# Gates taken out of PSUM by tanh and product, scores held 2^7 larger, and gate transposes moved into another PSUM tile, in a two-layer streaming encoder step

## The chip, the cores and the metric

The kernel runs on one core of one Trainium2 chip. A core has five engines that work side by side, each on its own queue of instructions in a fixed order: TensorE (PE in the profile; its weight loads are shown apart as PEld), VectorE (DVE), ScalarE (ACT), GpSimd (POOL), and SyncE (SP), which here issues the transfers (DMA). TensorE writes its results to PSUM, a small memory of banks, from where ScalarE and VectorE read them; everything else lies in SBUF. The metric is the device time of one execution in microseconds (us); the time given for a kernel is the median over its runs.

## The reference

Two layers run one after the other over a prompt of 2048 tokens and a sample of 64 tokens (width 1024, heads of 64). Each layer is, cut to what matters:

```python
h = rms_norm(x, norm_g)
q, k, v, gate = split(h @ w_in)                 # one combined projection
q, k = rms_norm per head (q, q_g), (k, k_g)
s = q @ k.T * 64 ** -0.5 + bias                 # own chunk of 64 and the chunks before it
p = softmax(s)                                  # layer A: with a sink per head in the sum
y = x + ((p @ v) * silu(gate)) @ w_out
```

Layer A has 16 query heads over 2 key/value heads and looks back 128 tokens; its bias is bucketed by distance. Layer B has 16 heads of each and looks back 512 tokens; its bias comes from a clipped distance. The outputs are the two results and the last rows of keys and values. silu(g) = g / (1 + exp(-g)) = 0.5 g (1 + tanh(g / 2)); the kernel uses the second form.

## The kernel before

All tokens are split into units of 256 (u0 to u7, two tiles of 128 each) and the sample as a unit of its own, which is taken ahead of the last one (`order`). Layer A works through its heads in four groups (qd 0 to 3), layer B through eight head pairs (hp 0 to 7), each over all units. A projection has its own PSUM tile (`project`, tag pj, a ring of two): chains of matmuls over eight blocks of the input, each with high and low parts of the operands, which come from ScalarE (copy) and VectorE (rest): `load_weights`, lines 467 and 470.

**The order of the work.** Attention is a pipeline over units, written out as steps: one step is the scores of one tile and one head (`scores`), and around it stands what is due. Between these the projections of later units are dealt out a few matmuls at a time (`filler.to`), so that TensorE always has something to do; the small works of a unit (head norms, gates, scans of the weights) stand in a list with a cost each (`Background`) and are handed out at each step (`bg.share`) or when the unit's scores need them. The order on each engine is then settled by a planner that simulates the program; each engine takes its queue in that order and waits on the others by semaphores.

**The gates.** When a projection is done, `evacuate` (layer A, 256 gate columns of 512) and `evacuate_b` (layer B, 128 of 512, for two tiles per unit) bring it out of PSUM. ScalarE copies queries and keys to `a` (tile pa; lines 702 and 715) with the token's scale, and the gate to tile pb (L702 also, and L723); in layer B it takes the values in between (L719, their rest on VectorE, L720). `head_norm` squares and sums queries and keys (GpSimd L756, VectorE L757 or L765, GpSimd L760, L761, and L769) and scales them (VectorE L774). `gate`, one of the works of the background list, then makes tanh(g/2) on ScalarE (L782) and (tanh + 1) g on VectorE (L783). In layer B the scale of the copy is C_B, one of three numbers per pair in `scl`, which `everywhere` spreads over the partitions from a row that `input_across` works out (the weights' largest values come from scans, L175).

**Attention in layer B, pairs 1 to 7.** Scores go to a PSUM tile with tag sb (1024 columns), a ring of two (L1416, L1417). One VectorE instruction per tile and head adds the bias and takes the minimum (L1420; the scores are held negative), ScalarE takes the exponent and its sum (L1429). The order in a unit is tile 0 and 1 of head 0, then of head 1. Head 0's probabilities are turned by a DMA transpose (`TURNED = (0,)`: ScalarE L1463 and GpSimd L1464 split them); head 1's on TensorE, one step after their scores, into another sb tile, from which ScalarE and VectorE take a high and a low part (`values`: L844 by way of `transpose`; L816, L817). I call these fillings PT01 (tile 0 of head 1) and PT11 (tile 1), and the scores' tiles S00, S10, S01, S11. Once the last row of a unit's sums is there, VectorE takes the reciprocal (L1437), multiplies head 0's part by PB (L1440) and GpSimd multiplies the gates by it into G (L1448, two instructions). Some steps later, in the rest of head 1's `products`, `gates` takes another sb tile, TensorE turns G into it (L844 again), ScalarE copies it with scale G_B (L1237), and `finish_pairs` multiplies it into the output (ScalarE L1247, VectorE L1249, GpSimd L1250). `store_kv` makes the output keys on GpSimd (L795). Pair 0 and layer A use another PSUM tile (tag tp) for the turned gates, and in layer A the scores' minimum is L1150.

**Constants.** `constants` loads the gains of queries and keys and works out their powers of two on VectorE: the keys' share `kf`, the queries' `qf`, while the weights of the first projection are being split.

Of the kernel before, what the change touches and what calls it, by code (L numbers as in the profile page):

```python
# [56 lines left out]
def hybrid_encoder_kernel(  # L57
# [71 lines left out]
    kf = const([P, 2], "kf")  # L129
    kgr = const([P, 2, 2 * HD], "kgr")  # L130
# [3 lines left out]
    held = {}  # L134

    def constants():
# [8 lines left out]
        nc.vector.tensor_tensor(qf, qsc, ksc, op=ALU.mult)  # L145
        nc.vector.tensor_scalar(kf.bitcast(I32), qf.bitcast(I32), 0x7F800000, None, op0=ALU.bitwise_and)
        nc.vector.tensor_scalar(kf, kf, 0.125, 1.0, op0=ALU.mult, op1=ALU.max)
        nc.vector.tensor_scalar(kf, kf, 2.0 ** 15, 1.0, op0=ALU.min, op1=ALU.mult)
        inv = t("ms", [P, 8])[:, 0:2]
        nc.vector.reciprocal(inv, kf)  # L150
        nc.vector.tensor_tensor(qf, qf, inv, op=ALU.mult)
        nc.vector.tensor_scalar(qf, qf, 60000.0, -60000.0, op0=ALU.min, op1=ALU.max)
# [5 lines left out]
    scl = const([P, 9, 3], "scl")  # L158
    gsb = const([P, 8, KC], "gsb")
    S_W, C_B, G_B = (lambda h, i=i: scl[:, h, i : i + 1] for i in range(3))  # L160
# [24 lines left out]
    def times(dst, a, c):  # L185
        nc.vector.tensor_scalar(dst, a, c, 1.0, op0=ALU.mult, op1=ALU.mult)

# [22 lines left out]
    def everywhere(h, o):  # L210
        ps = psum("tp", 512, 1)
        nc.tensor.matmul(ps[:, 0:3], ones[0:1, 0:1].to_broadcast([1, P]), o, start=True, stop=True)
        nc.vector.tensor_copy(scl[:, h], ps[:, 0:3])
# [6 lines left out]
    def input_across(h):  # L220
        across(h, h + 1)
        e, r, o = row[:, 16:17], row[:, 17:18], row[:, 20:23]
        powers(row[:, h : h + 1], e, r)
        times(o[:, 0:1], r, WB_)
        times(o[:, 1:2], e, 1 / (HB * WB_))
        times(o[:, 2:3], e, 0.5 / VB if h > 0 and len(TURNED) == 2 else 0.5 / (VB * PB))

    def input_scales(h):
        everywhere(h, row[:, 20:23])
        nc.vector.tensor_scalar(gsb[:, h], gain[:, 1, :], S_W(h), 1.0, op0=ALU.mult, op1=ALU.mult)  # L230
# [57 lines left out]
    def bias_vectors_a():  # L288
# [4 lines left out]
        nc.vector.tensor_scalar(va[:16, :VL], ps[:16, :VL], -1.0, 1.0, op0=ALU.mult, op1=ALU.mult)  # L293

    def bias_vectors_b():
# [5 lines left out]
            vb[:16, 127:383], vr[:16, 0:256], vr[:16, 0:1], -1.0, op0=ALU.subtract, op1=ALU.mult  # L301
        )

# [118 lines left out]
    bg = Background()  # L422

# [185 lines left out]
    rr = [const([P, NT + 1], f"rms{l}") for l in range(2)]  # L609

# [8 lines left out]
    def sums_to_scales(layer, tt, parts, ps):  # L619
# [12 lines left out]
        )  # L632

# [12 lines left out]
    def row_scales(unit):  # L646
# [18 lines left out]
        nc.gpsimd.tensor_tensor(rr[0][:, tt : tt + w], v[:, :w], mhalf[:, :w], op=ALU.pow)  # L665

# [21 lines left out]
    def evacuate(layer, tt, n, ps, C, G, b=None):  # L688
        a = t("pa", [P, 384], 4)
        pieces = [(a[:, : C - G], ps[:, : C - G])]  # L690
        if G:
            out = a
            if b is None:
                b = t("pb", [P, 256], 5)
                out = a, b
            pieces.append((b[:, :G], ps[:, C - G : C]))
        else:
            out = a
        sc = rr[layer][:, tt : tt + 1]
        for dst, src in pieces:  # L700
            if n == P:
                held["evac"] = nc.scalar.activation(dst, src, AF.Identity, scale=sc).ins  # L702
            else:
                nc.scalar.activation(dst[:n], src[n:], AF.Identity, scale=sc[n:])
        if n < P:
            for dst, src in pieces:
                nc.vector.scalar_tensor_tensor(
                    dst[:n], src[:n], sc[:n], dst[:n], op0=ALU.mult, op1=ALU.add
                )
        return out  # L710

    def evacuate_b(hp, tt, ps, g):
        a = t("pa", [P, 384], 4)
        true = a if tt >= NT - 4 else a[:, 0:256]
        nc.scalar.activation(true, ps[:, : true.shape[1]], AF.Identity, scale=C_B(hp))  # L715
# [7 lines left out]
        held["evac"] = nc.scalar.activation(g, ps[:, 384:512], AF.Identity, scale=C_B(hp)).ins  # L723
# [122 lines left out]
    halves = [slice(0, 64), slice(64, 128)]  # L846

# [1074 lines left out]
```

## Time and profile before

| what | value |
|---|---|
| runs | 2204.73, 2210.4 and 2212.95 us; median 2210.4 us |
| profiled execution | 2214.94 us |
| its span, first to last instruction | 2213.1 us (1.8 us lie around it) |
| TensorE busy | 2102.7 us, 95% |
| VectorE, ScalarE, GpSimd busy | 1563.9 (71%), 1425.7 (64%), 1004.9 us (45%) |
| TensorE's granted clock, mean | 0.991 |
| layer A, projections and attention | 6 to about 690 us; first scores at 47.3 |
| layer A's output projection | about 650 to 885 us |
| layer B, pair 0 | about 885 to 1050 us |
| layer B, pairs 1 to 7 | about 1050 to 2065 us |
| layer B's output projection | to 2209 us |

How the lines are read: a group of instructions shows its line in the kernel, its engine, its operation, output tile <- input tiles, shape and count, then busy time and mean ns of one, then the idle time of the engine ahead of them and who ended it. A row of waits shows engine, tile and line, "<-" the engine, tile and line that it waited for, and total us, number, longest us. A row of the timeline shows start, duration, engine, line and operation, and in brackets the idle time before it and who ended that. A row of a stretch shows the length, and for PE, PEld, DVE, ACT and POOL the busy time and the number of instructions, then granted clock, DMA share and GB/s.

### The profile page before, as it was taken

The page shows a single profiled execution, that of the slowest core. Times are in us where ns is not written, and L with a number is a line of the kernel's source. Part 1 is how long each engine was busy: PE and PEld are TensorE (multiplying, and loading weights), DVE is VectorE, ACT ScalarE, POOL GpSimd, SP SyncE. Part 2 cuts the span into 40 slices and gives each one's busy share as a digit, 9 for nine tenths or more (in the row PEclk, how much of TensorE's full clock was granted, in tenths as well). Part 3 has the DMA queues.
Part 4 walks back from the last instruction along what each step waited for, and adds up shares of the span by engine and source line. Part 5 has one row for each costly group of instructions (what it writes and reads, how often), then busy time and mean ns, then how long its engine had stood idle before and what let it go on. Part 6 is the DMA issues. An engine that isn't in the chain of part 4 may idle for free. (4 is left out here: it accounts for less than half of the span.)

```text
span 2213.1 us, 41369 instructions
## 1 busy us (share of the span) xinstructions
PE 2102.7 (95%) x13441; PEld 1522.1 (69%) x13441; DVE 1563.9 (71%) x4105; ACT 1425.7 (64%) x3610; POOL 1004.9 (45%) x1509
## 2 busy tenths in 40 slices
PE   7999999999999999989999999999999998998999
PEld 6887888788889997556555555555555555556888
DVE  6769777677676456778676777877767778677642
ACT  6878878777785333666666766766667667576420
POOL 5645544334454455853444444444454445443000
PEclk9999999999999999999999999999999999999999
DMA  8856546856546667545465565654756546345664
GB/s 274 275 162 215 179 127 219 234 160 195 170 129 184 210 204 244 171 143 167 107 186 133 130 177 130 173 148 121 186 133 155 159 111 172 91 104 136 199 200 124
DMA packets 383096, 372.87 MB, mean 168 GB/s; under 512 B 174672, under 2 KB 320352, under 8 KB 382848
## 3 DMA queue, kind: packets, MB, share of 16 engines
q1 hardware_dynamic: 382880, 370.23, 58.0%
q8 instruction: 106, 1.74, 0.3%
q14 instruction: 110, 0.90, 0.1%
HBM read 257.59 MB, written 73.43 MB: 150 GB/s over the span
## 5 line engine op out<-in xcount | busy, mean ns | idle before, releaser
L679 PE MATMUL pj<-wh,xx 128*128 128x512 f16 (+2 forms) x1648 | 643.4, 390 | 5.8 <-ACT pb L702 4.1
L681 PE MATMUL pj<-wh,xx 128*128 128x512 f16 (+2 forms) x1648 | 625.5, 380 | 2.5 <-POOL xx L564 2.5
L680 PE MATMUL pj<-wh,xx 128*128 128x512 f16 x1024 | 391.5, 382 | 0.0
L1429 ACT ACTIVATE p<-p,nm 128x640 f32<-128x640 f32 (+5 forms) x264 | 198.9, 753 | 213.6 <-DVE nm L1420 108.0
L1765 PE MATMUL pj<-xx,wh 128*128 128x264 f32 (+1 forms) x1024 | 290.0, 283 | 8.5 <-DVE res L1775 4.1
L1766 PE MATMUL pj<-xx,wh 128*128 128x264 f32 (+1 forms) x1024 | 287.7, 281 | 0.0
L1464 POOL TENSOR_TENSOR values<-p,values 128x640 f16<-128x640 f32 (+2 forms) x112 | 140.0, 1250 | 243.5 <-ACT values L1463 243.5
L680 PE MATMUL pj<-wl,xx 128*128 128x512 f32 (+1 forms) x624 | 233.9, 375 | 2.2 <-DVE wl L470 2.2
L564 POOL TENSOR_TENSOR xx<-xraw,xx 128x528 fp32r<-128x528 f32 (+4 forms) x144 | 184.9, 1303 | 87.8 <-ACT xx L563 74.6
L1420 DVE CUSTOM_DVE_ANT_0 p<-sb,BT 128x640 f32<-128x640 f32 (+5 forms) x272 | 195.6, 719 | 38.3 <-PE sb L1417 35.6
L1250 POOL TENSOR_TENSOR o<-gt,o 128x256 f32<-128x256 f32 (+1 forms) x132 | 101.1, 766 | 206.2 <-ACT p L1156 89.6
L761 POOL TENSOR_TENSOR f<-f,mhalf 128x4 f32<-128x4 f32 (+2 forms) x187 | 187.0, 1000 | 13.8
L681 PEld LDWEIGHTS <-xx 128*128 128x128 f16 x1024 | 100.9, 99 | 125.9 <-issue 3.9
L774 DVE TENSOR_TENSOR pa<-pa,f 128x256 f32<-128x256 f32 (+3 forms) x221 | 136.5, 618 | 55.1 <-POOL f L761 50.6
L1156 ACT ACTIVATE p<-p,nm 128x257 f32<-128x257 f32 (+2 forms) x272 | 134.3, 497 | 50.1 <-DVE nm L1150 41.7
L756 POOL TENSOR_TENSOR sq<-pa 128x256 f32<-128x256 f32 (+2 forms) x187 | 123.7, 663 | 72.5 <-ACT pa L715 38.2
L679 PEld LDWEIGHTS <-xx 128*128 128x128 f16 x1024 | 101.0, 99 | 71.5 <-issue 2.7
L680 PEld LDWEIGHTS <-xx 128*128 128x128 f16 x1024 | 100.9, 99 | 70.3 <-issue 2.9
L817 DVE SCALAR_TENSOR_TENSOR pl<-sb,ph 128x640 f16<-128x640 f32 (+4 forms) x144 | 106.2, 737 | 58.2 <-ACT ph L816 56.5
L1767 PE MATMUL pj<-xx,wl 128*128 128x264 f32 x512 | 145.0, 283 | 1.0 <-DVE wl L463 1.0
L1767 PE MATMUL pj<-xx,wh 128*128 128x264 f16 x512 | 142.1, 277 | 1.3 <-DVE wh L460 1.3
L1150 DVE CUSTOM_DVE_ANT_0 p<-sa,BT,nsink 128x256 f32<-128x256 f32 (+2 forms) x272 | 117.3, 467 | 34.6 <-PE sa L844 29.5
(273 smaller groups left out, 5290.7 us busy)
## 6 DMA issues: line engine op xcount, KB each, us to landing
xx<-xsb SPq DMA_DIRECT2D x112, 512.0 KB, 4.2
xx<-xsa SPq DMA_DIRECT2D x88, 512.0 KB, 4.8
xraw<-oga SPq DMA_DIRECT2D x64, 264.0 KB, 3.6
xraw<-ogb SPq DMA_DIRECT2D x64, 264.0 KB, 3.6
xsa<-xx SPq DMA_DIRECT2D x32, 512.0 KB, 4.0
scan<-in_w_in_b_dram SPq DMA_DIRECT2D x64, 256.0 KB, 4.6
wl<-in_w_in_b_dram SPq DMA_DIRECT2D x64, 256.0 KB, 4.0
xraw<-in_x_dram SPq DMA_DIRECT2D x40, 256.0 KB, 3.9
```

The costliest lines, as they stand in the source:

```text
L564: nc.gpsimd.tensor_tensor(lo, rv, wide(hi), op=ALU.subtract)
L679: nc.tensor.matmul(ps[:n, :C], xh, wh, start=k == 0, stop=False)
L680: nc.tensor.matmul(ps[:n, :C], xh, wl, start=False, stop=False)
L681: nc.tensor.matmul(ps[:n, :C], xl, wh, start=False, stop=k == KC - 1)
L761: nc.gpsimd.tensor_tensor(fv, fv, mhalf[:n, :H], op=ALU.pow)
L774: nc.vector.tensor_tensor(sv, sv, fv.unsqueeze(2).to_broadcast([n, H, HD]), op=ALU.mult)
L1420: mi = nc.vector.tensor_tensor_reduce(out=p[r, :nk], in0=S[r, o : o + nk], in1=b, op0=ALU.add, op1=ALU.min, scale=1.0, scalar=3e38, accum_ ...
L1429: ex = nc.scalar.activation(p[:n, :nk], p[:n, :nk], AF.Exp, scale=-1.0, bias=it.nm[:n, c : c + 1], accum_out=it.sm[:n, c : c + 1],)
L1464: lo = nc.gpsimd.tensor_tensor(two[:, :, 1, :], pv, two[:, :, 0, :], op=ALU.subtract)
L1765: nc.tensor.matmul(ps[:, :OT], wh, oh, start=k == 0, stop=False)
L1766: nc.tensor.matmul(ps[:, :OT], wh, ol, start=False, stop=False)
L1767: nc.tensor.matmul(ps[:, :OT], wl, oh, start=False, stop=k == KC - 1)
```

## The change

It has three parts.

1. Gates. In full tiles, `evacuate` and `evacuate_b` no longer copy the gate: a new `gate_of` takes tanh on ScalarE straight from PSUM, and VectorE multiplies (tanh + 1), or (tanh - 1) in layer A, with the PSUM tile into its place. In layer A the token scale is then missing; half of its negative (`nhalf`) is the tanh's scale, and the reciprocal sums `sm` are multiplied by the token scale and -1. In layer B, `scl` has a fourth number H_B, and C_B squared goes into G_B. `evacuate_b` does the gate first, then the copy to pa, then the values. The background work `gate` remains for the sample alone.
2. Scores. Queries are scaled by `up`, at most 2^7, a power of two found from the gains (the gains are loaded a second time, to every partition, 128x4, 256 KB); the biases are scaled by -up (`nup`), and the minimum instructions scale by `down` = 1/up from a [P, 1] pointer in place of the number 1.0. The factor PB goes into `scl` once per pair, and the multiplication after the reciprocal (L1440) goes.
3. Gate transposes of pairs 1 to 7. They go from the rest of the products, where they had an sb tile of their own, to the filling PT11, ahead of its transposes of probabilities, in columns 640 to 895 of the same tile; the copy (`gate_t`) follows the split of the probabilities.

```diff
+    def gate_of(ps, scale, g, one=1.0):
+        W = g.shape[1]
+        e = t("e", [P, 256], 1)[:, :W]
+        held["evac"] = nc.scalar.activation(e, ps, AF.Tanh, scale=scale).ins
+        nc.vector.scalar_tensor_tensor(g, e, one, ps, op0=ALU.add, op1=ALU.mult)
...
+        if n == P:
+            held["evac"] = nc.scalar.activation(a[:, : C - G], ps[:, : C - G], AF.Identity, scale=sc).ins
+            if G:
+                gate_of(ps[:, C - G : C], nhalf[:, tt : tt + 1], b[:, :G], -1.0)
+            return (a, b) if G else a
...
     def evacuate_b(hp, tt, ps, g):
         a = t("pa", [P, 384], 4)
         true = a if tt >= NT - 4 else a[:, 0:256]
+        gate_of(ps[:, 384:512], H_B(hp), g)
         nc.scalar.activation(true, ps[:, : true.shape[1]], AF.Identity, scale=C_B(hp))
...
-        held["evac"] = nc.scalar.activation(g, ps[:, 384:512], AF.Identity, scale=C_B(hp)).ins
         return a
...
+        both = t("res", [P, 2 * OT], 2)[:, : 4 * P].rearrange("p (d c) -> p d c", c=4)
+        load(both, qk_gain.partition_broadcast(P))
+        nc.vector.tensor_tensor(both[:, :, 0:2], both[:, :, 0:2], both[:, :, 2:4], op=ALU.mult)
+        nc.vector.tensor_reduce(
+            up, both[:, :, 0:2].rearrange("p d c -> p c d"), axis=AX.X, op=ALU.max,
+            apply_absolute_value=True,
+        )
+        exponent(up, up)
+        nc.vector.tensor_scalar(up, up, 2.0 ** 10, 1e-20, op0=ALU.mult, op1=ALU.max)
+        nc.vector.reciprocal(up, up)
+        nc.vector.tensor_scalar(up, up, 2.0 ** 29 * 2.0 ** 7, 2.0 ** 7, op0=ALU.mult, op1=ALU.min)
+        nc.vector.reciprocal(down, up)
+        times(nup, up, -1.0)
+        nc.vector.tensor_tensor(qsc, qsc, up, op=ALU.mult)
...
-                        op0=ALU.add, op1=ALU.min, scale=1.0,
+                        op0=ALU.add, op1=ALU.min, scale=down[:n, 0:1],
...
             nc.vector.reciprocal(sm[:n], sm[:n])
+            if n == P:
+                nc.vector.tensor_scalar(
+                    sm, sm, rr[0][:, tt : tt + 1], -1.0, op0=ALU.mult, op1=ALU.mult
+                )
...
-                    op0=ALU.add, op1=ALU.min, scale=1.0, scalar=3e38, accum_out=it.nm[r, c : c + 1],
+                    op0=ALU.add, op1=ALU.min, scale=down[r, 1:2], scalar=3e38, accum_out=it.nm[r, c : c + 1],
...
-                if turned(it, 0) and len(TURNED) == 1:
-                    part = it.sm[:n, TURNED[0] : w : 2]
-                    nc.vector.tensor_scalar(part, part, PB, 1.0, op0=ALU.mult, op1=ALU.mult)
...
+            gates_too = u != NU and it.hp > 0 and (i, h) == (1, 1)
+            if gates_too:
+                GT = PT[:, 5 * P : 5 * P + T]
+                for e, (_, g0, _) in enumerate(tiles):
+                    transpose(GT[:, g0 : g0 + n], it.G[:n, e * P : (e + 1) * P])
             for c in range(m):
                 transpose(PTv[:, (kb + c) % 5, :n], it.p[i, h][:n, c * P : (c + 1) * P])
...
+            if gates_too:
+                it.gt = gate_t(GT.rearrange("p (j s) -> p j s", j=1), T, G_B(it.hp))
...
             def rest():
-                if h == 1:
+                if h == 1 and it.hp == 0:
                     gates(it)
```

89 lines of the change are left out of this document (51 added, 38 removed).

## The prediction

> **What bounds the kernel now.** I read the first part of the page for the busiest engine, then the same engine by stage, then what its idle time ended on, and last, in the timeline, the places where it stops.
>
> ```profile
> span 2213.1 us, 41369 instructions
> PE 2102.7 (95%) x13441; PEld 1522.1 (69%) x13441; DVE 1563.9 (71%) x4105; ACT 1425.7 (64%) x3610; POOL 1004.9 (45%) x1509
> ```
>
> TensorE is busy for 95% of the span; the next engine, VectorE, for 71%. The change leaves the number and the shapes of the matmuls and transposes as they are, so it can only move TensorE's waits: 2213.1 - 2102.7 = 110 us, 6.4 of it before the first matmul and 3.8 behind the last. By stretches (layer A's beginning; layer B's head pair 0; its pairs 1 to 7):
>
> ```profile
> 0.00:200.00 200.00, 182.15 (x1091) 153.45 (x1092) 143.90 (x518) 155.05 (x415) 112.10 (x169) 0.98 0.73 231
> 885.00:1050.00 165.00, 152.81 (x932) 92.10 (x931) 131.40 (x300) 109.04 (x272) 94.96 (x127) 0.99 0.50 160
> 1050.00:2065.00 1015.00, 957.52 (x5976) 583.81 (x5975) 757.11 (x1948) 682.65 (x1705) 470.18 (x704) 0.99 0.55 142
> ```
>
> The columns are the length, then busy time and count of PE, PEld, DVE, ACT and POOL, and the granted clock (0.98 to 0.99 throughout). TensorE is idle 17.8 us in the first stretch, 12.2 in pair 0, and 57.5 in pairs 1 to 7, some 8 per pair. That last is the most there is to win where most of the change lies. What ended TensorE's waits, as total, times, longest:
>
> ```profile
> PE sb L844 <- DVE nm L1420: 14.0, 7, 2.3
> PE sb L1416 <- DVE nm L1420: 12.7, 10, 1.7
> PE tp L844 <- DVE pa L774: 11.0, 8, 1.7
> PE sb L844 <- DVE pl L817: 10.2, 14, 1.4
> PE pj L679 <- ACT pb L702: 4.1, 3, 2.1
> PE sb L844 <- ACT gt L1237: 1.5, 3, 0.9
> ```
>
> **1. Gates out of PSUM (evacuate, evacuate_b).** Before: ScalarE copies the gate to SBUF (L702, L723), later a tanh in SBUF (L782) and a VectorE product of two SBUF tiles (L783). After: tanh straight from PSUM, and a product that reads PSUM.
>
> ```profile
> L783 DVE SCALAR_TENSOR_TENSOR pb<-sq,pb 128x128 f32<-128x128 f32 x128 | 55.6, 434 | 20.5 <-ACT sq L782 20.3
> L723 ACT ACTIVATE pb<-pj,scl 128x128 f32<-128x128 f32 x128 | 46.6, 364 | 63.7 <-DVE values L720 60.9 <-DVE scrow L202 1.2
> L782 ACT ACTIVATE sq<-pb 128x128 f32<-128x128 f32 x128 | 38.4, 300 | 0.6
> L720 DVE SCALAR_TENSOR_TENSOR values<-pj,values 128x128 f16<-128x128 f32 x128 | 36.5, 285 | 2.9 <-ACT values L719 1.4
> L702 ACT ACTIVATE pb<-pj,rms 128x256 f32<-128x256 f32 x64 | 30.1, 470 | 0.0
> L782 ACT ACTIVATE sq<-pb 128x256 f32<-128x256 f32 x64 | 26.8, 419 | 2.8 <-DVE f L765 1.6
> L1237 ACT ACTIVATE gt<-sb,scl 128x256 f32<-128x256 f32 x56 | 26.2, 467 | 0.3
> ```
>
> I take the PSUM tanh at the price of the copy that it replaces, so ScalarE loses the L782 groups: 38.4 + 26.8 = 65 us. The product from PSUM is nearest to L720 (one PSUM and one SBUF input, 285 ns); L783 costs 434 because it varies from 258 to 1514 ns:
>
> ```profile
> L783 DVE SCALAR_TENSOR_TENSOR pb<-sq,pb x204: 258/411/1514, 35.0 to 2014.1; 128x128 f32<-128x128 f32 x64, 128x256 f32<-128x256 f32 x32, 128x64 f32<-128x64 f32 x4, 64x256 f32<-64x256 f32 x2
> L720 DVE SCALAR_TENSOR_TENSOR values<-pj,values x128: 268/286/293, 873.6 to 2009.4; 128x128 f16<-128x128 f32 x128
> ```
>
> So VectorE saves 128 x 0.149 = 19 us in layer B (bounds 0 and 19). [...]
>
> Neither engine sets the end, so the 65 and 19 us are worth only what they take from TensorE's waits (3 below). Against them stands a later release. In layer A the projection's PSUM tile (pj, two in a ring) now goes free behind a VectorE product instead of a ScalarE copy: 256 wide some 0.42 us, and up to one other VectorE instruction (0.6) ahead of it, +0.4 to +1.2. TensorE already waits there (row L679 <- L702: 4.1 us in 3) while head norms and projections come densely, up to 200 us; later such tiles are 3 us and more ahead. 3 waits x 0.6, and some 1 us at places that are now just covered: **+3 (0 to +6)**. The 17 small halvings on POOL and 64 scalings of sm on VectorE (L1440's kind, 178 ns) lie beside other work: 0.
>
> In layer B the order becomes tanh, product, pa copy, V; before it was pa copy, V, gate. The row of L723 shows that two readers of a pj tile take turns: ScalarE stood 60.9 us, 55 times, behind VectorE's L720 on the same tile. So the pa copy starts 0.36 (tanh) + 0.29 (product) + up to 0.6 (VectorE's queue) = 0.65 to 1.25 later; were both engines free to read, 0.36. [...]
>
> What hangs on pa are head norm, the tp transposes, and the scores. The chain has slack in most units; not at a pair's last unit, whose second tile stops TensorE (L844 <- L774, 11.0 us in 8). There VectorE itself stands behind a scan's transfer:
>
> ```profile
> 1327.06 0.29 DVE L783 SCALAR_TENSOR_TENSOR pb<-sq,pb 128x128 f32<-128x128 f32 x1 [0.46 <-ACT sq L782]
> 1329.36 0.69 DVE L175 TENSOR_REDUCE most<-scan 128x1 f32<-128x512 f32 x1 [2.01 <-DMA scan<-in_w_in_b_dram]
> 1330.93 0.84 DVE L1249 TENSOR_TENSOR o<-o,o 64x256 f32<-64x256 f32 x2
> ```
>
> L774 follows L175, so a later pa is covered by those 2.01 us; in the changed order two L1249 (0.84 together) come ahead of the second L774 and one L783 (0.28) goes: **+0.5 per pair (0 to +0.9)**. Pair 0, where VectorE is busy for 131 of 165 us: **0 (-3 to +3)**, its lighter queue against its later pa.
>
> **2. Scores 2^7 larger (scale=down).** The minimum instructions take the scale from a pointer. The nearest rows are the two layers' own forms: L1150 already has one pointer more than L1420.
>
> ```profile
> L1150 DVE CUSTOM_DVE_ANT_0 p<-sa,BT,nsink 128x128 f32<-128x128 f32 x16 | 5.0, 346 | 2.4 <-PE sa L844 1.5 <-POOL f L769 0.9
> L1420 DVE CUSTOM_DVE_ANT_0 p<-sb,BT 128x128 f32<-128x128 f32 x16 | 4.6, 285 | 10.1 <-PE sb L1417 10.1
> L1440 DVE TENSOR_SCALAR sm<-sm 128x2 f32<-128x2 f32 x56 | 10.0, 178 | 1.3
> ```
>
> 61 ns each (0 to 61), x 256 in layer B = 16 us of VectorE, against 10.0 for L1440, which goes (PB is put into scl once per pair), and the 19 above: VectorE is about 13 us lighter in layer B.
>
> The beginning is different. The constants load 256 KB more (both), ahead of the weights on the SP queue, and VectorE gets two instructions of 256 elements and a net six tiny ones, in a stretch in which TensorE waits for VectorE's weight halves:
>
> ```profile
> 15.18 0.16 DVE L152 TENSOR_SCALAR qf<-qf 128x2 f32<-128x2 f32 x1
> 16.91 0.41 DVE L591 TENSOR_TENSOR o<-res 128x256 f32<-128x256 f32 x1
> 27.39 0.50 PE L680 MATMUL pj<-wl,xx 128*128 128x512 f32 x1 [2.19 <-DVE wl L470]
> 47.29 0.26 PE L1139 MATMUL sa<-KA,q 128*128 128x128 f16 x1 [3.86 <-ACT values L789]
> ```
>
> 2 x 0.41 + 6 x 0.16 = 1.8 us, which go straight to TensorE, whose waits of 2.19 and, ahead of the first scores, 3.86 us stand behind this stretch; a late transfer can add as much again where VectorE waits for it, and idle moments can hide half: **+3 (+1 to +5)**.
>
> **3. Gate transposes into the filling of PT11 (pairs 1 to 7).** Before, each unit used the ring of two sb tiles 7 times, the gate's (then L1237 on ScalarE) among them; after, 6 times. The waits for L1237 go (1.5 us in 3): **-0.2 per pair**. The new wait: the transposes stand at the front of the filling with the unit's last probabilities, one step behind its last scores, and need G, two POOL products behind the reciprocal. How early is G today? In order, a unit 1, 3, 4 and 5 of one pair:
>
> ```profile
> 1225.37 0.76 POOL L1448 TENSOR_TENSOR G<-pb,sm 128x128 f32<-128x128 f32 x2 [1.45 <-DVE sm L1440]
> 1226.22 0.60 PE L844 MATMUL sb<-ident,p 128*128 128x128 f32 x4
> ...
> 1258.74 1.29 POOL L1448 TENSOR_TENSOR G<-pb,sm 128x128 f32<-128x128 f32 x2 [1.59 <-DVE sm L1440]
> 1260.68 0.76 PE L844 MATMUL sb<-ident,p 128*128 128x128 f32 x5 [1.05 <-DVE pl L817]
> ...
> 1276.90 0.46 POOL L795 TENSOR_TENSOR ko<-pa,kgr 128x128 f32<-128x128 f32 x1 [0.58 <-DVE pa L774]
> 1277.53 0.76 POOL L1448 TENSOR_TENSOR G<-pb,sm 128x128 f32<-128x128 f32 x2 [0.17 <-PE sb L844]
> 1276.73 0.71 PE L844 MATMUL sb<-ident,p 128*128 128x128 f32 x5
> ...
> 1291.80 1.01 POOL L761 TENSOR_TENSOR f<-f,mhalf 128x4 f32<-128x4 f32 x1
> 1293.45 1.39 POOL L1448 TENSOR_TENSOR G<-pb,sm 128x128 f32<-128x128 f32 x2
> 1295.47 0.74 PE L844 MATMUL sb<-ident,p 128*128 128x128 f32 x5 [2.31 <-DVE nm L1420]
> ```
>
> G ends 0.09 us ahead of the filling in unit 1 (1226.13 against 1226.22), 0.65 in unit 3, 0.63 in unit 5, and 1.56 behind it in unit 4 (1278.29 against 1276.73). With L1440 gone G comes some 0.2 earlier. In unit 4 the changed order puts G ahead of L795 on POOL, which takes off 0.46 + 0.17 more: a wait of about **+0.7 per pair (0 to +1.6)**.
>
> In unit 5, 2.31 us end on scores whose PSUM tile frees late, since ScalarE reaches the copy of the tile (L816) with a backlog; of that one L1237 (0.47) and one L782 (0.30) go. But G is only 0.63 + 0.2 ahead there: no more than 0.83 can be won of the 2.31, and in unit 3 no more than 0.85 of its 1.05, since then the filling waits for G. I take **-0.7** in unit 5 and **-0.4** in unit 3. The gate's copy now stands behind VectorE's L817 of the same tile, which holds the tile some 0.5 longer; its next user comes 3 us later: 0.
>
> **Sum.** Per pair +0.5 - 0.2 + 0.7 - 0.7 - 0.4 = -0.1, over 7 pairs -1 (-13 to +12). Beginning +3, layer A +3, pair 0 0: **+5**. The profiled execution took 2214.9 us (span 2213.1 and 1.8 around it) and would be 2220; the median of the runs is 4.5 lower, 2210.4, so I predict **2215**.
>
> **Rivals.**
> - **G is late (slower).** If VectorE's pointers (61 ns x 4 per unit) eat what L1440 gives back, and L795 still stands ahead, unit 4 waits the whole 1.56: net +0.75 a pair, 5 us, +6 elsewhere, 11 over the median; from that point on it decides. Half a microsecond later still adds 0.4 each in units 1 and 7 and 0.5 in unit 4; one POOL power instruction ahead of G (1.01 us) makes 5.5 a pair. In between, some 3.5 x 7 + 6 = +30: **2240**. For it: POOL takes turns with long instructions; against it: in the other units POOL already waits for L1440 (the bracketed 1.45 and 1.59) and so would start G sooner.
> - **The relief pays (faster).** ScalarE's 65 and VectorE's 13 us take the waits in units 3 and 5 down to where G stops them, 0.85 + 0.83, and gt's 0.2: 1.9 x 7 = 13, and the beginning costs only 1: **2198**. It needs G in unit 4 to be in time, 1.56 earlier; the rows give 0.8 to 1.0.
> - **pa's lateness shows.** Unit 7 +0.9 x 7, pair 0 +4, layer A +6, beginning +3: **2229**. For it: the turns on the pj tile; against: the 2.01 us of the scan that cover it.
> - **Nothing shows**: all beside TensorE, **2210**.
>
> **Chances.** Forecast 0.46 (own range 2204 to 2226), G late 0.22, relief 0.17, pa 0.10, nothing 0.05. Half a per cent, 11 us, is about what a measurement of this kernel can tell from no change. From the cases: slower 0.05 + 0.20 + 0.07 = 0.32, faster 0.16, within 0.52. The range takes the relief and half of G late: **2194 to 2238**.
>
> **What would show it.** Right: L782's 128-wide groups gone, the product near 285 ns with a small spread, no TensorE wait for gt, a wait of TensorE's sb transposes for POOL's G once per pair (unit 4) near 0.7, pj waits in the first 200 us longer by 2 to 4, and the first scores later than 47.3 us by 2 to 4. Wrong: G waits in most units (slower), or pairs 1 to 7 idle under 45 us (faster).

## The result, and the profile after

The changed kernel takes 2224.5 us (median of six runs, 2221.1 to 2227.9) against 2209.1 us for the kernel before (six runs, 2204.7 to 2213.3): a ratio of 1.0068, 95% interval 1.0049 to 1.0086, so 15 us slower. The predicted 2215 was 9.5 us short, and the range held the time.

The page of the changed kernel begins:

```profile
span 2223.7 us, 41231 instructions
PE 2107.8 (95%) x13441; PEld 1526.4 (69%) x13441; DVE 1573.5 (71%) x4146; ACT 1384.1 (62%) x3418; POOL 997.2 (45%) x1518
```

TensorE has the same 13441 instructions and is as full as before; ScalarE has 192 fewer. The waits of TensorE, as total, times, longest:

```profile
PE tp L884 <- DVE pa L814: 22.1, 8, 8.7
PE sb L1460 <- DVE nm L1464: 11.6, 15, 1.7
PE tp L884 <- DVE scl L236: 8.4, 5, 1.7
PE sb L884 <- POOL G L1489: 6.2, 15, 0.5
PE sb L884 <- DVE pl L857: 6.0, 7, 1.8
PE pj L717 <- DVE pb L730: 3.9, 4, 1.5
PE sb L884 <- DVE nm L1464: 3.6, 2, 2.0
```

Against the rows before: the waits on the head norm (pa) doubled from 11.0 to 22.1 us, with one of 8.7 among them; a small copy (scl) went from 1.3 to 8.4; G is new with 6.2; the waits for the turned tile's release (L884 <- L1464, 14.0 before) and for pl (10.2) shrank; gt's is nearly gone.

Where the time went, stage by stage, from the start times of TensorE's instructions in the two traces (a stage runs from its first scores to the next stage's, the last one to the start of the last matmul; "idle" is the sum of TensorE's gaps over 0.06 us in it, "rest" is its length less that):

| stage | before: idle + rest, us | after: idle + rest, us | change, us |
|---|---|---|---|
| to the first scores | 13.7 + 33.6 | 15.2 + 37.9 | +5.8 |
| layer A, to its last scores | 9.4 + 620.7 | 10.8 + 619.3 | 0.0 |
| to pair 0's first scores | 10.8 + 203.3 | 9.5 + 205.9 | +1.3 |
| pair 0 | 12.2 + 148.1 | 20.6 + 152.2 | **+12.5** |
| pairs 1 to 7, to the last scores | 57.5 + 942.3 | 52.8 + 938.6 | -8.4 |
| to the last matmul | 3.1 + 154.4 | 2.7 + 154.1 | -0.7 |

The stages sum to +10.5 us, the difference of the two profiled executions. The other 5 us of the median are not in them: the profiled execution of before was 5.9 us above its median of six, that of after 1.0.

**Pair 0.** Here lies nearly all of the growth of the waits on the head norm. In pair 0 alone, before and then after:

```profile
PE tp L844 <- DVE pa L774: 1.4, 2, 0.9
PE tp L884 <- DVE pa L814: 12.4, 2, 8.7
```

The two waits of the changed kernel are 8.73 us and, 21 us later, 3.69 us. The timeline of the changed kernel at the longer one, GpSimd first, then VectorE and TensorE:

```profile
902.95 0.80 POOL L796 TENSOR_TENSOR sq<-pa 128x256 f32<-128x256 f32 x1
906.33 1.27 POOL L591 TENSOR_TENSOR xraw<-xraw,rows 128x512 f32<-128x512 f32 x1 [2.59 <-DMA xraw<-x]
907.56 1.15 POOL L595 TENSOR_TENSOR xx<-xraw,xx 128x512 f16<-128x512 f32 x1
908.67 0.20 POOL L800 TENSOR_TENSOR f<-f,small 128x4 f32<-128x4 f32 x1
908.82 3.37 POOL L595 TENSOR_TENSOR xx<-xraw,xx 128x512 f16<-128x512 f32 x3
912.14 1.01 POOL L801 TENSOR_TENSOR f<-f,mhalf 128x4 f32<-128x4 f32 x1
913.19 0.83 DVE L814 TENSOR_TENSOR pa<-pa,f 128x256 f32<-128x256 f32 x1 [3.59 <-POOL f L801]
914.16 0.66 PE L884 MATMUL tp<-ident,pa 128*128 128x128 f32 x2 [8.73 <-DVE pa L814]
```

The head norm's two small steps (L800, L801; 1.2 us together) stand on GpSimd behind a product that waits 2.6 us for its transfer and among four conversions of the next units' input. The input of this head norm is late before that: its copy to pa starts 2.05 us after the tanh, which now stands in its place, because the product between them waits 1.16 us for its turn on VectorE:

```profile
898.77 0.37 ACT L729 ACTIVATE e<-pj,scl 128x128 f32<-128x128 f32 x1 [0.23 <-PE pj L719]
900.30 0.28 DVE L730 SCALAR_TENSOR_TENSOR pb<-e,pj 128x128 f32<-128x128 f32 x1
900.82 0.46 ACT L756 ACTIVATE pa<-pj,scl 128x256 f32<-128x256 f32 x1
```

In the kernel before the same head norm's two steps were issued ahead of the product that waits for its transfer, and of the conversions:

```profile
893.67 1.44 POOL L560 TENSOR_TENSOR xraw<-xraw,rows 128x512 f32<-128x512 f32 x1
895.08 0.24 POOL L760 TENSOR_TENSOR f<-f,small 128x4 f32<-128x4 f32 x1
895.40 1.01 POOL L761 TENSOR_TENSOR f<-f,mhalf 128x4 f32<-128x4 f32 x1
897.12 1.27 POOL L560 TENSOR_TENSOR xraw<-xraw,rows 128x512 f32<-128x512 f32 x1 [0.72 <-DMA xraw<-x]
898.35 4.76 POOL L564 TENSOR_TENSOR xx<-xraw,xx 128x512 f16<-128x512 f32 x4
```

The wait costs twice, since slower work follows it. These are stretches of the changed kernel, with the granted clock third from the right:

```profile
898.00:905.00 7.00, 6.76 (x37) 3.57 (x35) 6.38 (x16) 3.22 (x11) 5.67 (x7) 1.00 0.81 264
905.00:914.00 9.00, 0.43 (x3) 0.14 (x1) 3.00 (x7) 2.55 (x7) 7.40 (x8) 0.67 0.61 176
914.00:917.00 3.00, 2.84 (x10) 1.43 (x11) 1.14 (x5) 2.11 (x6) 1.08 (x2) 0.50 1.06 397
917.00:920.00 3.00, 3.00 (x14) 1.64 (x13) 2.92 (x7) 0.43 (x2) 0.13 (x1) 0.77 0.39 140
920.00:930.00 10.00, 10.00 (x63) 5.95 (x61) 7.25 (x19) 5.79 (x16) 6.35 (x7) 1.00 0.01 2
```

After the idle stretch TensorE's granted clock is 0.50 until about 918.4 us (0.77 over the 3 us from 917), and 1.00 from there on. Of pair 0's +12.5 us, 8.4 are idle time and 4.1 are slower work. The 4.2 us at 0.50 behind the long wait cost some 2.1 of these (an estimate from the clock: half of them). Two more such stretches lie further on in the changed kernel's pair 0, at 935 to 939 behind the second wait and at 1010 to 1018 (mean clock 0.57 in both); the kernel before has one:

```profile
917.00:922.00 5.00, 5.00 (x21) 2.75 (x22) 3.37 (x9) 4.42 (x13) 2.96 (x5) 0.66 0.88 280
```

Two of the changed kernel's stretches follow the waits of 8.73 and 3.69 us, and the third begins in a wait of 2.46 us that ends at 1011.95; the stretch of the kernel before follows no wait over 1.5 us in the 12 us ahead of it. What brings the clock down is not shown by these runs.

**Pairs 1 to 7.** One new wait is the copy of scl. In the changed kernel, then in the one before:

```profile
1408.21 1.61 DVE L814 TENSOR_TENSOR pa<-pa,f 128x256 f32<-128x256 f32 x1 [1.40 <-POOL f L801]
1409.74 0.15 DVE L236 COPY scl<-tp 128x4 f32<-128x4 f32 x1
1409.94 0.66 PE L884 MATMUL tp<-ident,pa 128*128 128x128 f32 x4 [1.66 <-DVE scl L236]
```

```profile
1391.00 0.16 DVE L213 COPY scl<-tp 128x3 f32<-128x3 f32 x1 [0.55 <-PE tp L212]
1391.85 1.61 DVE L774 TENSOR_TENSOR pa<-pa,f 128x256 f32<-128x256 f32 x1 [0.69 <-POOL f L761]
```

The copy of 0.15 us, which frees the one tp tile, has come to stand behind a head norm. The other waits of the same pair, after, are those of unit 4 and unit 5:

```profile
1433.52 0.32 PE L1460 MATMUL sb<-KA,q 128*128 128x384 f16 x1 [1.13 <-DVE nm L1464]
1436.24 0.69 PE L884 MATMUL sb<-ident,G 128*128 128x128 f32 x2 [0.51 <-POOL G L1489]
...
1451.05 0.32 PE L1460 MATMUL sb<-KA,q 128*128 128x384 f16 x1 [0.36 <-DVE nm L1464]
1453.32 0.33 PE L884 MATMUL sb<-ident,G 128*128 128x128 f32 x1 [0.26 <-POOL G L1489]
1454.12 0.33 PE L884 MATMUL sb<-ident,G 128*128 128x128 f32 x1 [0.48 <-POOL G L1489]
```

Unit 3's 1.05 is gone, unit 4's 1.72 is 1.13, and unit 5's 2.31 is 1.10 in three pieces, two of them for G.

### The profile page after: what moved, and what is told of

It is laid out like the page before. It is cut to its first block, busy times and chain, and to the rows that moved or that the text cites. A ratio compares the mean times of both kernels' runs of the same rounds, so it can differ in the third digit from the quotient of the medians.

```text
span 2223.7 us, 41231 instructions
## 1 busy us (share of the span) xinstructions
PE 2107.8 (95%) x13441; PEld 1526.4 (69%) x13441; DVE 1573.5 (71%) x4146; ACT 1384.1 (62%) x3418; POOL 997.2 (45%) x1518
## 4 chain that ended last, share of the span: by engine, by line
PE 62%; DVE 14%; ACT 7%; DMA 6%; issue 5%; POOL 5%; SPq 1%; ACTq 0%; POOLq 0%; DVEq 0%
PE pj L717 10%; PE pj L719 10%; PE pj L718 10%; PE pj L1813 4%; PE pj L1815 4%; PE pj L1814 4%; PE sb L884 2%; DVE p L1464 2%; DMA scan<-in_w_in_b_dram 2%; PE tp L884 2%; PE sa L884 2%; PE o L1648 2%; DVE pa L814 2%; PE sb L1460 1%; PE sb L1461 1%
## 5 line engine op out<-in xcount | busy, mean ns | idle before, releaser
L717 PE MATMUL pj<-wh,xx 128*128 128x512 f16 (+2 forms) x1648 | 643.0, 390 | 6.4 <-DVE pb L730 3.9
L1464 DVE CUSTOM_DVE_ANT_0 p<-sb,BT,down 128x640 f32<-128x640 f32 (+5 forms) x272 | 212.1, 780 | 34.7 <-PE sb L1461 32.5
L801 POOL TENSOR_TENSOR f<-f,mhalf 128x4 f32<-128x4 f32 (+2 forms) x187 | 186.7, 998 | 13.6
L796 POOL TENSOR_TENSOR sq<-pa 128x256 f32<-128x256 f32 (+2 forms) x187 | 119.1, 638 | 158.5 <-ACT pa L756 92.7
L1196 ACT ACTIVATE p<-p,nm 128x257 f32<-128x257 f32 (+2 forms) x272 | 134.5, 497 | 69.6 <-DVE nm L1190 56.2
L814 DVE TENSOR_TENSOR pa<-pa,f 128x256 f32<-128x256 f32 (+3 forms) x221 | 126.1, 571 | 57.6 <-POOL f L801 51.8
L717 PEld LDWEIGHTS <-xx 128*128 128x128 f16 x1024 | 101.1, 99 | 71.7 <-issue 2.7
L1190 DVE CUSTOM_DVE_ANT_0 p<-sa,BT,nsink 128x256 f32<-128x256 f32 (+2 forms) x272 | 134.4, 528 | 21.9 <-PE sa L884 18.0
```

What stands on the lines that cost most here:

```text
L717: nc.tensor.matmul(ps[:n, :C], xh, wh, start=k == 0, stop=False)
L801: nc.gpsimd.tensor_tensor(fv, fv, mhalf[:n, :H], op=ALU.pow)
L814: nc.vector.tensor_tensor(sv, sv, fv.unsqueeze(2).to_broadcast([n, H, HD]), op=ALU.mult)
L1464: mi = nc.vector.tensor_tensor_reduce(out=p[r, :nk], in0=S[r, o : o + nk], in1=b, op0=ALU.add, op1=ALU.min, scale=down[r, 1:2], scalar=3e3 ...
```

## The experiments

The kernels below were measured later than the result, on two chips, beside runs of the kernel before, which took 2219.4, 2221.3 and 2219.1 us there against 2209.1. So the ratios to before count, and where an expectation names a time, it is to be read against 2209. From the traces I use the idle time of TensorE by stage as in the table above. In pairs 1 to 7 it is the better measure, since the rest of that stage, with the same 5840 instructions, went from 938 to 951 us from one trace to the next. **before_again** is the kernel before, unchanged:

> The kernel before once more, for a profile taken on the chip of the three runs beside it: chips differ by some 10 us (medians of the kernel before of 2209 and 2219 us), so that delays by stage are only read within one chip. Every theory expects the time of the kernel before.

It took 2220.5 us, and its trace has 11.4 us idle in pair 0 and 56.8 in pairs 1 to 7 (12.2 and 57.5 in the first trace), so that in these two traces idle time repeats to about a microsecond. Up to layer A's last scores it is 7 us longer than the first trace, behind them 1.6 us shorter. The measured ratios and stages in one table:

| kernel | ratio to before, 95% interval | pair 0, idle + rest | pairs 1 to 7, idle |
|---|---|---|---|
| changed | 1.0068, 1.0049 to 1.0086 | 20.6 + 152.2 | 52.8 |
| gate_last | 1.0040, 1.0025 to 1.0055 | 9.3 + 147.4 | 61.8 |
| pow_first | 1.0020, 1.0008 to 1.0033 | 15.6 + 150.7 | 52.7 |
| up_const | 1.0039, 1.0024 to 1.0054 | 20.5 + 151.9 | 55.1 |
| own_tile | 1.0090, 1.0061 to 1.0118 | 20.8 + 151.9 | 62.4 |
| move_only | 1.0044, 1.0029 to 1.0059 | 12.3 + 148.1 | 67.9 |
| gates_only | 1.0072, 1.0056 to 1.0088 | 20.5 + 151.3 | 62.2 |
| scores_only | 1.0013, 0.9998 to 1.0028 | 10.5 + 147.3 | 57.5 |
| p0_gate_last | 0.9971, 0.9954 to 0.9988 | 10.3 + 147.5 | 53.8 |
| two | 0.9954, 0.9937 to 0.9971 | 8.8 + 149.8 | 48.1 |
| three | 0.9938, 0.9920 to 0.9957 | 9.6 + 149.7 | 47.6 |
| two_g | 0.9911, 0.9889 to 0.9933 | 8.4 + 150.2 | 44.1 |

**gate_last**: the gate behind the other copies, in all pairs.

```diff
 def evacuate_b(hp, tt, ps, g):
-        gate_of(ps[:, 384:512], H_B(hp), g)
...
             vh[:, :, HD:P], v, c, vh[:, :, 0:HD], op0=ALU.mult, op1=ALU.subtract
         )
+        gate_of(ps[:, 384:512], H_B(hp), g)
         return a
```

> The changed kernel, with the gate's tanh and product in layer B put behind the copies of queries, keys and values, as the gate stood before the change. Theory (GpSimd's order in pair 0): the copy to pa comes about 1 us later in the changed kernel, and with it GpSimd's order puts a head norm's last step behind three conversions of the next units' input; that is one wait of 8.7 us, and most of what pair 0 lost (delay 7.1 us at its first scores, 19.5 at pair 1's). With pa first the head norm stands ahead of the conversions again: pair 0 loses 0 to 3 in place of 12.4, and the kernel takes 2212 to 2216 us, 9 to 12 less than the changed one. Rival (the tile's readers take turns, in whatever order; or the minimum with a pointer makes VectorE late in pair 0): the order of gate and pa doesn't matter, pair 0 still loses 9 to 13, and the time stays at 2222 to 2227. In pairs 1 to 7 both expect a change under 3 us.

Pair 0's loss is gone (9.3 us idle, 147.4 of rest), as the theory said. But the kernel is only some 6 us faster than the changed one: in pairs 1 to 7 the idle time rose by 9, which neither side expected. There unit 5's wait is back in one piece, 2.37 us ending at 1443 us of its trace, although ScalarE is as light as in the changed kernel. The lighter ScalarE alone does not remove that wait. What the order of gate and pa does to the order of the queues in these pairs was not followed further.

**pow_first**: the place on GpSimd by itself, with gate first.

```diff
+                    low = nc.gpsimd.tensor_tensor(lo, rv, wide(hi), op=ALU.subtract)
+                    if rows is not None and "pow" in held:
+                        behind(low.ins, held["pow"])
...
+                held["pow"] = nc.gpsimd.tensor_tensor(fv, fv, mhalf[:n, :H], op=ALU.pow).ins
```

> The changed kernel, gate first in every pair, with one order added on GpSimd: the conversions of the next units' input in pair 0 (L595) stand behind the power step of the latest head norm (L801). Theory (GpSimd's order makes the 8.7 us wait in pair 0): the three conversions, 3.4 us, leave their place ahead of the power step; one product that waits 2.6 us for its transfer still stands ahead. The wait falls to 4 to 5.5 us, pair 0's idle time from 20.6 to 14 to 17 us, and the kernel is 0.3% to 0.5% slower than before. Rival (pa itself is late, by the turns on the PSUM tile): the wait stays at 8 us or more, and the kernel 0.6% to 0.75% slower.

The wait falls from 8.73 to 4.95 us and pair 0's idle time to 15.6, both within what the theory named, at 0.2% over before, better than it named:

```profile
906.01 1.26 POOL L591 TENSOR_TENSOR xraw<-xraw,rows 128x512 f32<-128x512 f32 x1 [2.58 <-DMA xraw<-x]
907.24 0.20 POOL L802 TENSOR_TENSOR f<-f,small 128x4 f32<-128x4 f32 x1
907.51 1.01 POOL L803 TENSOR_TENSOR f<-f,mhalf 128x4 f32<-128x4 f32 x1
908.49 4.67 POOL L595 TENSOR_TENSOR xx<-xraw,xx 128x512 f16<-128x512 f32 x4
910.07 0.66 PE L886 MATMUL tp<-ident,pa 128*128 128x128 f32 x2 [4.95 <-DVE pa L816]
```

pa is as late as in the changed kernel (2.3 us behind pair 0's first scores in both, 0.2 in the kernel before), so GpSimd's order is shown to be the cause of 3.8 of the 8.7 us; the second wait falls too, from 3.69 to 1.45. That the rest of the long wait comes from the product that waits for its transfer ahead of the head norm is read from the rows, not tested by itself; that all of it hangs on the late pa is shown by gate_last, where it is gone.

**up_const**: the beginning.

```diff
-        load(both, qk_gain.partition_broadcast(P))
...
-        nc.vector.reciprocal(down, up)
-        times(nup, up, -1.0)
+        nc.vector.memset(up, 2.0 ** 7)
+        nc.vector.memset(down, 2.0 ** -7)
+        nc.vector.memset(nup, -(2.0 ** 7))
```

> The changed kernel, with up, down and nup set to 2^7, 2^-7 and -2^7 by memsets (the values that the gains of this case give) in place of the second load of the gains and the chain that works them out; this leaves out the guard for large gains. Theory: the beginning's loss (first scores at 53.05 us against 47.29) is this chain: VectorE waits 1.3 us for the load, its tiny steps stand between the weight halves, and the bias row that needs their result comes 7 us later, 26.7 us against 18.9, with TensorE waiting behind it. The first scores come at 47 to 49 us, and the kernel takes 2218 to 2221 us, 4 to 6 less than the changed one. Rival: the beginning is late by the gates of layer A (PSUM tile freed by the product): the first scores stay at 51.5 us or later, and the time at 2222 or more.

The first scores come at 49.4 us in place of 53.1, and the ratio is 0.3% lower, with intervals that just meet. In the changed kernel VectorE waits for the second load, and the bias row follows its result:

```profile
16.42 0.43 DVE L158 TENSOR_TENSOR res<-res 128x256 f32<-128x256 f32 x1 [1.29 <-DMA res<-in_qk_gain_dram]
26.69 0.60 DVE L140 TENSOR_SCALAR row<-tp,nup 16x383 f32<-16x383 f32 x1
```

With constants the row comes at 19.5 (18.9 before). The second trace of the kernel before had its first scores at 49.4 itself. Over all traces of this case, the eight kernels with the chain have their first scores at 51.4 to 53.5 us, the six without it at 47.3 to 50.4. So the chain costs some 3 to 4 us, and the remaining 2 us of the 5.8 are within what the execution changes. Of the 5.8 only 1.5 are idle time: from 30 to 34 us the granted clock is 0.50 in the changed kernel, 1.00 in the kernel before.

**own_tile, move_only, gates_only, scores_only**: the parts apart. own_tile is the changed kernel with the turned gates' own tile as before:

```diff
-            gates_too = u != NU and it.hp > 0 and (i, h) == (1, 1)
...
-            GT = psum("tp", 512, 1)
+            GT = psum_b("sb", 1024, 2) if it.hp and len(TURNED) else psum("tp", 512, 1)
...
-                if h == 1 and it.hp == 0:
+                if h == 1:
                     gates(it)
```

> The changed kernel with the gate's transposes in an sb tile of their own again, in the rest of head 1's products; all else as changed. Theory: in pairs 1 to 7 the changed kernel is 1.3 us a pair shorter than before, some 9 us, and most of it is the sixth in place of the seventh filling of the ring: with the old place the seven pairs take 5 to 9 us more, 2229 to 2234 us in all, and TensorE waits for gt again. Rival: the gain is the relief of ScalarE and VectorE by the gates out of PSUM; then the seven pairs take within 3 us of the changed kernel's, 2222 to 2228, since the waits for G (6.2 us in the changed kernel) go in return.

9.6 us more idle time in pairs 1 to 7, and 0.22% slower than the changed kernel by the ratios, whose intervals overlap. By the idle time the shared tile pays, within the rest of the change, as the theory said; by the time alone the rival is not excluded. The waits that return are not gt's, as the theory had it (1.0 us in one wait), but those of the scores on the ring's release (L1460 <- L1464, 11.6 to 17.1 us) and those for pl (4.9 to 12.7). move_only puts the same move into the kernel before:

> The kernel before, with only the gate's transposes moved into the filling of the last turned probabilities. Theory: as for the old place: the seven pairs take 4 to 8 us less than before, nothing changes ahead of pair 1, and the kernel takes 2201 to 2206 us. Rival (the relief of ScalarE is what pays): with L1440 still between the reciprocal and G, and ScalarE's load as before, the waits for G (7 to 12 us) take back what the tile gives: within 3 us of the kernel before or slower, 2207 to 2214.

```diff
+                for e, (_, g0, _) in enumerate(tiles):
+                    transpose(GT[:, g0 : g0 + n], it.G[:n, e * P : (e + 1) * P])
             for c in range(m):
...
-                if h == 1:
+                if h == 1 and it.hp == 0:
                     gates(it)
```

Slower by 0.44%, with 10 us more idle time in pairs 1 to 7. The theory is wrong, and the rival's G is not the reason; these waits are, where before had 1.3 and 4.0:

```profile
PE tp L844 <- DVE scl L213: 11.2, 5, 2.2
PE tp L197 <- DVE KB L1371: 8.4, 6, 3.7
```

Both end waits on the single tp tile, which a small step on VectorE frees. In all five waits for scl its copy stands right behind a head norm's 1.61 us (L774), as in the changed kernel; in the kernel before it stood ahead of it. Without these two rows the idle time would be some 4 us below before's (48.3 against 52.2), so the move may well pay by itself, but it doesn't in this order. gates_only is the kernel before with `gate_of`, `nhalf`, the four scales per pair and the new `evacuate` and `evacuate_b`; of the diff, the lines

```diff
+        gate_of(ps[:, 384:512], H_B(hp), g)
...
-        held["evac"] = nc.scalar.activation(g, ps[:, 384:512], AF.Identity, scale=C_B(hp)).ins
...
-                    it.todo += head_norm(n, pr[:n, 0:256]) + gate(n, it.gate[:n, e])
+                    it.todo += head_norm(n, pr[:n, 0:256])
```

> The kernel before with only the gates taken out of PSUM by tanh and product (gate first in layer B; no change to the scores, to L1440 or to the place of the gate's transposes). Theory: pair 0 loses some 12 us by GpSimd's order, as in the changed kernel; the beginning loses nothing (it was the constants); in pairs 1 to 7 the lighter ScalarE alone gives back 0 to 4: 8 to 13 us slower than before, 0.4% to 0.6%. Rival (relief of ScalarE and VectorE is the gain of pairs 1 to 7): they give back 6 to 10, and it is 2 to 6 us slower than before.

Pair 0's loss is all here (20.5 + 151.3), so the gates' part carries it. Pairs 1 to 7 are 5 us worse, not better: the scl copy is late here too (10.5 us in 5), and the kernel is 0.72% slower, more than either side named. But without the waits for scl the idle time is 51.7 us against before's 56.2: the lighter engines may give back some 4 us, which the late copy more than takes. The runs don't part the two. scores_only is the kernel before with the new constants and

```diff
-                    op0=ALU.add, op1=ALU.min, scale=1.0, scalar=3e38, accum_out=it.nm[r, c : c + 1],
+                    op0=ALU.add, op1=ALU.min, scale=down[r, 1:2], scalar=3e38, accum_out=it.nm[r, c : c + 1],
...
-                    nc.vector.tensor_scalar(part, part, PB, 1.0, op0=ALU.mult, op1=ALU.mult)
```

> The kernel before with only the scores 2^7 larger (constants, minimum with a pointer) and PB in scl. Theory: the first scores come 3 to 6 us later; pair 0 keeps the old order on GpSimd and loses nothing; the pointer's price is small (L1464 within 20 ns of L1420 where VectorE waits for nothing) and lies beside TensorE: 0.1% to 0.35% slower than before. Rival (61 ns each on VectorE is on the path from scores to tile): idle time of pairs 1 to 7 at 64 us or more, 0.5% slower or more.

0.13%, which its interval does not tell from no change, and within 2 us the same idle time as before in pair 0 and in pairs 1 to 7, though each minimum takes 60 ns more on VectorE (876 ns against 817 at 128x640). The theory's price was wrong (it named 20 ns at most), its place right: beside TensorE.

**p0_gate_last, three, two, two_g**: what the causes are worth together. p0_gate_last moves the gate back in pair 0 alone:

```diff
-        gate_of(ps[:, 384:512], H_B(hp), g)
+        if hp:
+            gate_of(ps[:, 384:512], H_B(hp), g)
...
             vh[:, :, HD:P], v, c, vh[:, :, 0:HD], op0=ALU.mult, op1=ALU.subtract
         )
+        if not hp:
+            gate_of(ps[:, 384:512], H_B(hp), g)
```

> The changed kernel, with the gate behind queries, keys and values in pair 0 alone; pairs 1 to 7 as changed. Theory: pair 0 no longer loses 12 us, and nothing else moves: 0 to 0.25% slower than before (0 to 5 us), the beginning's 5.8 less what pairs 1 to 7 gain. Rival (gate first is what pairs 1 to 7 live on, but the gain and the loss come in one through the common order of the queues): the gain of pairs 1 to 7 goes as well, 0.35% to 0.5% slower.

Pair 0 is at 10.3 + 147.5, pairs 1 to 7 at the changed kernel's, and the kernel is 0.29% faster than before: better than expected. The step from 1.0068 to 0.9971 is 21 us, and pair 0 accounts for 15; the other 6 are about what the two intervals leave open. two adds the copy of scl on ScalarE, three also the constants, which leaves out the guard for large gains; two_g is two with the order in the filling turned round:

```diff
-        nc.vector.tensor_copy(scl[:, h, :w], ps[:, :w])
+        nc.scalar.copy(scl[:, h, :w], ps[:, :w])
```

```diff
-                for e, (_, g0, _) in enumerate(tiles):
-                    transpose(GT[:, g0 : g0 + n], it.G[:n, e * P : (e + 1) * P])
             for c in range(m):
                 transpose(PTv[:, (kb + c) % 5, :n], it.p[i, h][:n, c * P : (c + 1) * P])
...
             while short:
                 short.pop(0)()
+            if gates_too:
+                for e, (_, g0, _) in enumerate(tiles):
+                    transpose(GT[:, g0 : g0 + n], it.G[:n, e * P : (e + 1) * P])
```

> The changed kernel with three mends together: the gate behind queries, keys and values in pair 0; up, down and nup as constants 2^7, 2^-7, -2^7 (the guard for large gains left out); and the copy of scl out of PSUM in everywhere on ScalarE in place of VectorE, since in the changed kernel TensorE waits 1.7 us per pair, 8.4 in all, for that small copy, which stands behind a head norm's L814 on VectorE. Theory: 12 + 4 + 6 to 8 us less than the changed kernel: 0.2% to 0.4% faster than before. Rival (the wait for scl is replaced by the next one, the head norm that VectorE does then): 0.1% faster to 0.1% slower.

> The changed kernel with two mends that leave nothing out: the gate behind queries, keys and values in pair 0, and the copy of scl on ScalarE. Theory: the idle time of pair 0 is 10 us and that of pairs 1 to 7 47 to 49 as with three mends, the beginning keeps its 2 to 4 us of constants: 0.4% to 0.6% faster than before. Rival (the small copy on ScalarE only paid with the early beginning's order): 0.25% to 0.35% faster, as with the gate's order alone.

> The two mends, and in the filling of the last turned probabilities the gate's transposes behind the probabilities' in place of ahead of them. Theory: TensorE's waits for G (6.2 us in 15) are the price of the front place, since the probabilities are there first; behind them G has 0.6 us more: the waits for G fall under 2 us, and the kernel is 3 to 5 us faster than with the two mends. Rival (the split of the probabilities then starts later, or the order of the queues moves): within 2 us of the two mends, or slower.

With the copy on ScalarE the wait for scl is 1.3 us (8.4 in the changed kernel) and the idle time of pairs 1 to 7 falls by 5 to 6 against p0_gate_last. three is 0.62% faster than before, above the 0.2% to 0.4% that its theory named, and two 0.46%, as its theory had it; the intervals of p0_gate_last, two and three overlap, so the copy's and the constants' shares are shown by the waits and not by the times. In two_g the waits for G fall too; two first, then two_g:

```profile
PE sb L887 <- POOL G L1492: 6.5, 15, 0.8
```

```profile
PE sb L887 <- POOL G L1492: 0.9, 3, 0.5
```

two_g is the fastest kernel of the case, 0.89% under before and by the ratios 1.6% under the changed one, with all of the computation in it. Its gain over two, some 10 us in the medians, is more than the theory's 3 to 5. The traces show 6 of it as idle time, 4 in pairs 1 to 7: of the 5.6 us less waiting for G part comes back at the scores (L1463 <- L1467, 10.4 us in two and 14.1 in two_g). In the other 4 us TensorE works; they are not explained.

## Why the prediction was right, and where it was not

The range held by its width and by luck: in the traces pair 0 came out 12.5 us above its term and pairs 1 to 7 some 7 below theirs, so that two errors took from each other. The likeliest case's own range (2204 to 2226) holds 2224.5 only at its edge, and a kernel slower by more than half a per cent had been given a chance of 0.32, against 0.52 for no such difference.

- **Bound and prices: right.** TensorE's instructions stayed. Besides its waits, the granted clock moved its time (4.1 us of slower work in pair 0, where it was 0.50 to 0.57 in three stretches), which the prediction had left out. The prices hold: tanh from PSUM 365 ns (364 taken), the product from PSUM 282 (285), 256 wide 418 (0.42 us), the spread of the product 266 to 424. The pointer costs 59 ns at 128x128 in layer B (344 against 285); what I missed is that layer A's form, which had one pointer, pays about the same for a second (407 against 346):

```profile
L1464 DVE CUSTOM_DVE_ANT_0 p<-sb,BT,down 128x128 f32<-128x128 f32 x16 | 5.5, 344 | 1.1 <-PE sb L1461 1.1
L1190 DVE CUSTOM_DVE_ANT_0 p<-sa,BT,nsink 128x128 f32<-128x128 f32 x16 | 5.9, 407 | 1.0 <-PE sa L884 0.9
L730 DVE SCALAR_TENSOR_TENSOR pb<-e,pj 128x128 f32<-128x128 f32 x128 | 36.0, 282 | 22.5 <-ACT e L729 21.4
L756 ACT ACTIVATE pa<-pj,scl 128x256 f32<-128x256 f32 x96 | 45.5, 474 | 59.8 <-DVE pb L730 57.5 <-DVE scrow L224 1.5
```

- **Beginning, +3 (+1 to +5)**: 3 to 4 by up_const; the size is right, and that the constants are the cause. That it all goes into TensorE's waits is not: they grew by 1.5 us of the 5.8, and the rest is slower work, where the granted clock was 0.58 from 27 to 30 us and 0.50 from 30 to 34 (1.00 in the kernel before).
- **Layer A, +3**: 0.0. The later release of pj is there (L717 <- L730: 3.9 us in 4), but it took the place of the old wait (4.1 in 3); the stage's idle time rose by 1.4 us and its other work fell by as much.
- **Pair 0, "0 (-3 to +3), its lighter queue against its later pa"**: the step that failed, by 12.5 us. That pa would be late behind the product was right (last row above: copies of this form wait 57.5 us for it), but its size was not: 0.65 to 1.25 us was worked out, with one other VectorE instruction ahead of the product; in the tile ahead of the long wait three stood there and it was 2.05, and the median over all 128 copies is 2.1. And I priced it as a delay of its own size, where its effect is that GpSimd's order puts other work ahead of the head norm: 8.73 us once and 3.69 once, with a clock of 0.50 and 0.57 behind them. The rival on pa had the mechanism's place with +4 for pair 0, a third of the measured.
- **Pairs 1 to 7, -0.1 per pair**: -0.7 in idle time (52.8 against 57.5; the other 3.7 of the 8.4 us lie in the rest, which was 938 to 951 us in the traces), or -0.84 in one pair that I followed wait by wait (6.91 to 6.07 us). Unit 3: -1.05 (-0.4 taken). Unit 4: +0.51 for G (+0.7 taken), and -0.6 at its first scores, not foreseen. Unit 5: -1.2 (-0.7 taken, and 0.83 as the most that G leaves: G came earlier too, and the waits for it that are left are 0.74). Last unit: +0.1 (+0.5 taken). The 0.9 us there, the upper end of that term and what the rival on pa takes seven times, is shown by no run: the copies to pa came 2.1 us behind the tanh (median), and the unit lost 0.1. And +1.41 for scl, which no step named: there the working followed the pieces that the change edits, not a small copy that the new order of VectorE put behind one of them.
- **The rivals.** "G is late" is real as a wait (6.2 us in 15) but not the decision. "The relief pays" is not borne out as a gain in time: gates_only and gate_last have the light ScalarE and more idle time in pairs 1 to 7 than before. Whether some 4 us of relief are hidden there behind the late copy of scl (10.5 and 9.2 us) stays open; a run of gates_only with that copy on ScalarE would tell.

What stays open: why the planner puts these orders out; only that they differ, and what they cost, is shown.

## What to carry to other kernels

Where a planner sets the order of each queue, price an instruction that comes later by what then stands ahead of it in the next queue, not by its lateness: here a copy that started 2.05 us behind the tanh ended in a wait of 8.73 us, 3.8 of them by GpSimd's order (pow_first). Look for the long instructions, and those waiting for transfers, on the queue that the late result goes through, and price the swap. When a change is slower, measure idle time by stage before undoing it: one place lost more than the whole change did (12.5 us against 10.5 between the profiled executions), and mending that place and two small ones made it 0.9% faster than before. Put the operand that comes last behind the others in a filling (waits for G of 6.5 us in two, 0.9 in two_g), and give a copy that frees a single-buffered PSUM tile to an engine whose queue has no long instruction ahead of it there (waits for scl of 8.4 us with its copy on VectorE, 1.3 on ScalarE).

## What was not expected of the hardware

Waits of TensorE of 8.73 and 3.69 us, and one of 4.95 us in pow_first, are followed by some 3 to 4 us at a granted clock near one half (0.50 from 914 to 917 us, 0.57 from 935 to 939; 0.50 from 910 to 913 in pow_first). But such a stretch also comes without a long wait: in the kernel before the mean clock is 0.66 from 917 to 922 us, with no wait over 1.5 us in the 12 us ahead of it. So the slower work of a stage can't be put down to one wait without looking at the clock of each stretch.
